# Sums of squares for a norm: adding the row blocks on VectorE before the product with ones, in the first pass of a streaming encoder step

## The chip, the cores and the metric

The kernel runs on one core of one Trainium2 chip. The metric is the device time of one execution in microseconds. TensorE (PE) multiplies matrices, VectorE (DVE), ScalarE (ACT) and GpSimd (POOL) work element by element, and SyncE (SP) issues the loads and stores (DMA).

## What is computed

The reference is one layer of a streaming encoder: 2048 prompt tokens and 8 x 16 sample tokens of width 1024. Each token is normalised, one projection feeds three groups of heads (forgetting attention, RWKV-7, cross-attention into 256 memory tokens), and a second projection brings the gated results back:

```
def rms_norm(x, g, eps=NORM_EPS):
    xf = x.astype(jnp.float32)
    y = xf * lax.rsqrt(jnp.mean(xf * xf, axis=-1, keepdims=True) + eps)
    return (y * g.astype(jnp.float32)).astype(x.dtype)
...
    h = rms_norm(x, norm_g) @ w_in
    fox_cols, rwkv_cols, mem_cols = jnp.split(h, [FOX_COLS, FOX_COLS + RWKV_COLS], axis=-1)
...
    y = x + o @ w_out
```

The change concerns `rms_norm` alone: how the sum of x² over the 1024 columns of a token is made.

## The kernel before

**Two phases.** The first (inside `with ExitStack() as p1`) goes over the tokens in four passes, `for it in range(4)`. Pass 0 takes 512 prompt tokens and the 128 sample tokens together, 640 columns; the passes 1 to 3 take 512 each. A pass normalises x (`prep_x`), projects it (`lora_in`, `shifted`, `wide`, `pair`), and runs the RWKV state update (`rwkv_in`, `rwkv_mid`, `rwkv_scan`, `rwkv_out`). The second phase does the two attentions and the output projection.

**The norm in pass 0.** x comes transposed, so that a tile holds 128 of the 1024 columns of x on its partitions and tokens along its free dimension; eight such row blocks (`raws[k]`, k = 0 to 7) make a token. `prep_x` goes over the 640 tokens in two parts, tokens 0 to 255 and 256 to 639 (`for t0, t1 in ((0, 2), (2, 5))`, in units of 128 tokens). For each part:

- L247 loads the blocks (SP; blocks 0 to 2 and 3 to 5 lie in two buffers of the weights' pool, tag `hl`; blocks 6 and 7 in the buffers `bk` and `bt`).
- L251 squares block k on ScalarE into the tile `xsq` (`sqs`).
- The product with `one1` (128 x 1 ones) on TensorE sums a block's squares over its 128 partitions. `xsq` is the stationary operand, so a product yields the sums of 128 tokens, one on each partition: column t of the PSUM tile `pq`. It is called through the helper `mm`, whose line is L59. Each fp32 product is two passes of TensorE in the trace.
- `rsqrt_small` makes the inverse root: scale and epsilon on VectorE (L68, out `rsq`), the power of -0.5 on GpSimd (L62).
- Products with `ident` spread the result over the partitions (`pb`, L59), and ScalarE copies it to `rb` (and, for the last 128 tokens, to `rb4`) at L269.
- For each block VectorE scales x by it and by the gain (L65, `xraw`), ScalarE rounds it to fp32r (L279, `xk`), and VectorE (even k) or GpSimd (odd k) forms the remainder (L62, `xk`). A value is kept as the sum of two such parts, and a projection takes three products for it.

Between the two parts the first weights are loaded (`between`): L200 loads, L201 rounds, GpSimd forms the remainder (`w`). The tiles of the pool `ws` with tag `hl`, four in all, hold these weights and, until the norm is done, also six of the eight blocks of x; the next weights (128x1024 for the columns k and r) go into the same four. `pjd` is the PSUM tile of the projections that `proj_d` makes. The passes 1 to 3 form the sums in another way (L261, ScalarE's accumulator over x in token order); the change doesn't touch these.

**What sets the order.** The program is written in one order, then put into another: `_arrange`, at the end of the kernel, gives each instruction a cost and its dependences, places all of the program's instructions on the five engines with a list scheduler that has fixed costs for each kind of instruction, for a slow array after a pause and for the buffers that a tile needs, and does so with three weights and six refinements of the ranks each. It keeps the order with the smallest computed total and sorts the whole program by it. Each engine then works through its instructions in that order, and waits for whatever each needs. Constant loads (L788, tile `craw`, with its conversions at L789) are part of the same order.

Of the kernel before, what the change touches and what calls it, by code (L numbers as in the profile page):

```python
# [17 lines left out]
KC = 8  # L18
# [33 lines left out]
def kernel(ctx: ExitStack, tc: tile.TileContext, I: dict, O: dict):  # L52
    nc = tc.nc
    V, S, G, PE, SY = nc.vector, nc.scalar, nc.gpsimd, nc.tensor, nc.sync
# [3 lines left out]
    def mm(out, lhsT, rhs, start=True, stop=True):  # L58
        PE.matmul(out, lhsT, rhs, start=start, stop=stop, skip_group_check=True)  # L59

    def tt(e, out, a, b, op):
        e.tensor_tensor(out=out, in0=a, in1=b, op=op)  # L62

    def stt(out, a, s, b, op0, op1):
        V.scalar_tensor_tensor(out=out, in0=a, scalar=s, in1=b, op0=op0, op1=op1)  # L65
# [9 lines left out]
    M, A_, SUB, MAX = ALU.mult, ALU.add, ALU.subtract, ALU.max  # L75
# [18 lines left out]
    def ct(name, shape, dtype=F32):  # L94
        return cp.tile(shape, dtype, tag=name, name=name)
# [15 lines left out]
    one1 = ct("one1", [128, 1])  # L111
# [6 lines left out]
    def rsqrt_small(out, ssum, n, scale, eps):  # L118
        ts(V, out, ssum, scale, eps, M, A_)
        tt(G, out, out, mhalf[:, :n], ALU.pow)  # L120


    with ExitStack() as p1:
# [93 lines left out]
        def spans(tok0, off, n):  # L217

            a = min(max(512 - off, 0), n)
            return [(o, m, t) for o, m, t in ((0, a, tok0 + off), (a, n - a, TP)) if m]  # L220

        def prep_x(tok0, n, xtok, xT, gcol, tiles=None, between=lambda: None):

            nt = n // 128
            first = n == 640
            ssq = sm.tile([128, 2, 8], F32, tag="ssq", name="ssq")
            rsq = sm.tile([128, 8], F32, tag="rsq", name="rsq")
            rb = xs_.tile([128, 512], F32, tag="rb", name="rb")
            rb4 = sm.tile([128, 512], F32, tag="nsq", name="rb4", bufs=1) if first else None
            xk, raws = [], []  # L230

            for t0, t1 in ((0, 2), (2, 5)) if first else ((0, nt),):
                c0, c1 = 128 * t0, 128 * t1
                if first:

                    m = c1 - c0
                    sqs = [rv.tile([128, 8, 256], F32, tag="gm", name="xsq", bufs=2)] if not t0 else [
                        rv.tile([128, 5, 384], F32, tag="gm", name="xsq", bufs=2), rv.tile([128, 3, 384], F32, tag="su", name="xsq2")]
                    pq = ps.tile([128, 512], F32, tag="ra", name="pq")
                    if not t0:  # L240
                        threes = [ws.tile([128, 2, 4, 256], F32, tag="hl", name="xraw").rearrange("p x a b -> p (x a b)")[
                            :, 0:1920].rearrange("p (k c) -> p k c", k=3) for _ in range(2)]
                        threes += [rv.tile([128, 1, 640], F32, tag=t_, name="xraw") for t_ in ("bk", "bt")]
                        raws = [threes[k // 3][:, k % 3] if k < 6 else threes[k - 4][:, 0] for k in range(KC)]
                    for j, k in enumerate((0, 3, 6, 7)):
                        for a, w, r0 in spans(tok0, c0, m):
                            SY.dma_start(threes[j][:, :, c0 + a:c0 + a + w],  # L247
                                         xT[128 * k:128 * (k + threes[j].shape[1]), r0:r0 + w].rearrange("(k p) t -> p k t", p=128))
                    for k in range(KC):
                        sq = sqs[k // 5 if t0 else 0][:, k % 5 if t0 else k, :]  # L250
                        S.activation(sq, raws[k][:, c0:c1], AF.Square)  # L251
                        for t in range(t1 - t0):
                            mm(pq[:, t:t + 1], sq[:, 128 * t:128 * t + 128], one1, start=k + t == 0, stop=k == KC - 1)
                    rsqrt_small(rsq[:, t0:t1], pq[:, 0:t1 - t0], t1 - t0, 1.0 / D, EPS)
                else:
                    for t in range(t0, t1):
                        r0 = tok0 + 128 * t
                        for j in range(2):
                            xt = xs_.tile([128, 512], F32, tag="xraw", name="xt", bufs=3)
                            SY.dma_start(xt, xtok[r0:r0 + 128, 512 * j:512 * j + 512])  # L260
                            S.activation(xt, xt, AF.Square, accum_out=ssq[:, j, t:t + 1])  # L261
                    tt(V, ssq[:, 0, :nt], ssq[:, 0, :nt], ssq[:, 1, :nt], A_)
                    rsqrt_small(rsq[:, t0:t1], ssq[:, 0, t0:t1], t1 - t0, 1.0 / D, EPS)
                pb = (ps if first else pj).tile([128, 512], F32, tag="ra" if first else "pj", name="pb")
                for t in range(t0, t1):
                    mm(pb[:, 128 * t - c0:128 * t - c0 + 128], rsq[:, t:t + 1].to_broadcast([128, 128]), ident)
                cuts = [(rb, 0, c0, min(c1, 512))] + ([(rb4, 512, 512, 640)] if c1 > 512 else [])
                for r_, o, a, b in cuts:
                    S.copy(r_[:, a - o:b - o], pb[:, a - c0:b - c0])  # L269
                for k in range(KC):  # L270
                    if not t0:
                        xk.append(tiles[k] if tiles else xs_.tile([128, 2, 640], F32R, tag="xk", name="xk", bufs=XKB))
                        if not first:
                            raws.append(xs_.tile([128, 512], F32, tag="xraw", name="xraw", bufs=3))
                            SY.dma_start(raws[k][:, :n], xT[128 * k:128 * (k + 1), tok0:tok0 + n])
                    raw, hl = raws[k], xk[k]
                    for r_, o, a, b in cuts:
                        stt(raw[:, a:b], raw[:, a:b], vec[:, gcol + k:gcol + k + 1], r_[:, a - o:b - o], M, M)
                    S.copy(hl[:, 0, c0:c1], raw[:, c0:c1])  # L279
                    tt(G if k % 2 else V, hl[:, 1, c0:c1], raw[:, c0:c1], hl[:, 0, c0:c1].bitcast(F32), SUB)  # L280
                if not t0:
                    between()
            return xk
# [566 lines left out]
        def memory_x():  # L850
            tiles = [rw.tile([128, 2, 256], F32R, tag=t_, name="xm") for t_ in ("e1", "e2", "e3", "e5", "xsk", "xsr")]
            tiles.append(rv.tile([128, 2, 256], F32R, tag="xsg", name="xm", bufs=2))
            tiles.append(rv.tile([128, 2, 256], F32R, tag="bv", name="xm", bufs=2))
            memx.extend(prep_x(0, 256, I["mem"], I["memT"], V_MG, tiles))
# [28 lines left out]
        for it in range(4):  # L883
            samp = it == 0
            tok0, n = 512 * it, 640 if samp else 512
            blocks = [(0, 256), (256, 384)] if samp else [(0, 512)]
            lora = []
            xk = prep_x(tok0, n, I["x"], I["xT"], V_G, between=lambda: lora.append(wd_load((LORA, 64), (FV + 384, 6))))
            lora_in(*lora, xk, blocks, it, tok0)
            if not it:  # L890
# [3 lines left out]
            nt, t0 = n // 128, 4 * it  # L894
# [1143 lines left out]
```

## Time and profile before

| | |
|---|---|
| three runs | median 1809.12 us (1807.52 to 1819.66) |
| the profiled execution | 1797.65 us |
| its span, first to last instruction | 1795.9 us |
| its mean granted TensorE clock | 0.972 |
| first start of a product with ones, last start | 4.6, 24.3 us |
| squares in pass 0 | 16 on ScalarE, 399 to 526 ns each |
| bytes moved in the first 60 us | 14.01 MB |

Times in the rows are microseconds from the start of the span unless marked ns. A row in order of time gives start, duration, engine, line, operation, out<-in with the tiles' names, shapes, how often it was merged, and in brackets how long the engine stood idle before it and what ended that. A row of a window gives the busy time of PE, of PE's weight loads, of DVE, ACT and POOL with their counts, then the granted clock (1.00 is full speed), the busy share of the DMA engines and the GB/s that they moved. A line in a row can be a helper's: L59 is every product, L62 every operation on two tensors, L65 and L68 those with a scalar.

### The profile page before, as it was taken

The page shows a single profiled execution, that of the slowest core. Times are in us where ns is not written, and L with a number is a line of the kernel's source. Part 1 is how long each engine was busy: PE and PEld are TensorE (multiplying, and loading weights), DVE is VectorE, ACT ScalarE, POOL GpSimd, SP SyncE. Part 2 cuts the span into 40 slices and gives each one's busy share as a digit, 9 for nine tenths or more (in the row PEclk, how much of TensorE's full clock was granted, in tenths as well). Part 3 has the DMA queues.
Part 4 walks back from the last instruction along what each step waited for, and adds up shares of the span by engine and source line. Part 5 has one row for each costly group of instructions (what it writes and reads, how often), then busy time and mean ns, then how long its engine had stood idle before and what let it go on. Part 6 is the DMA issues. An engine that isn't in the chain of part 4 may idle for free.

```text
span 1795.9 us, 41000 instructions
## 1 busy us (share of the span) xinstructions
PE 1696.7 (94%) x16313; PEld 1362.8 (76%) x16313; DVE 978.1 (54%) x2295; ACT 897.9 (50%) x1783; POOL 811.8 (45%) x824
## 2 busy tenths in 40 slices
PE   7989999999999999999899999799999899999998
PEld 6989989687887788886688887466667666667776
DVE  4654655572454564354574372776745765675214
ACT  5424343523243524233324343588898778886552
POOL 3654543242322242131132151477788566866552
PEclk8999999999999999999999999799999999999999
DMA  6763846653644654644635654534445772444432
GB/s 196 267 202 117 269 144 206 209 178 120 212 156 142 244 184 159 198 155 140 204 109 168 195 160 132 166 121 154 128 149 169 251 251 89 138 142 157 154 111 106
DMA packets 236314, 303.11 MB, mean 169 GB/s; under 512 B 81594, under 2 KB 185976, under 8 KB 220250
## 3 DMA queue, kind: packets, MB, share of 16 engines
q1 hardware_dynamic: 236122, 300.49, 51.5%
q8 instruction: 128, 2.10, 0.5%
q14 instruction: 64, 0.52, 0.1%
HBM read 210.15 MB, written 90.28 MB: 167 GB/s over the span
## 4 chain that ended last, share of the span: by engine, by line
PE 37%; DMA 7%; DVE 7%; ACT 7%; issue 2%; POOL 2%; SPq 1%; DVEq 0%; POOLq 0%; ACTq 0%
PE py L59 8%; PE po L59 6%; PE pjd L59 6%; PE pS L59 5%; PE pjt L59 3%; PE pm L59 2%; ACT P L1143 1%; DMA inv_d<-yt 1%; ACT Ph L1146 1%; POOL Pl L62 1%; DMA sp_d<-spr 1%; DMA xd<-inv_d 1%; DMA rb<-rd 1%; PE pz L59 1%; PE sc L59 1%
## 5 line engine op out<-in xcount | busy, mean ns | idle before, releaser
L59 PE MATMUL pjd<-xk,w 128*128 128x512 f32 (+4 forms) x2280 | 540.2, 378 | 13.0 <-ACT xk L279 4.6
L59 PEld LDWEIGHTS pjd<-xk,w 128*128 128x128 f32 (+1 forms) x2280 | 386.5, 192 | 80.8 <-issue 10.5
L62 POOL TENSOR_TENSOR Pl<-P,Ph 128x512 fp32r<-128x512 f32 (+3 forms) x272 | 318.8, 1183 | 160.6 <-ACT Ph L1146 132.8
L59 PE MATMUL pjt<-w,xk 128*128 128x256 f32 x2040 | 291.4, 290 | 3.9 <-issue 3.9
L59 PEld LDWEIGHTS pjt<-w,xk 128*128 128x128 f32 x2040 | 265.6, 192 | 10.1 <-issue 4.1
L59 PE MATMUL py<-W,oh 128*128 128x512 f32 x816 | 242.6, 399 | 0.9 <-ACT W L1331 0.4
L1143 ACT ACTIVATE P<-pS,NB 128x512 f32<-128x512 f32 x240 | 147.5, 624 | 87.1 <-PE pS L59 34.4
L59 PEld LDWEIGHTS py<-W,oh 128*128 128x128 f32 x816 | 150.9, 189 | 40.1 <-issue 1.0
L59 PE MATMUL pS<-Q,K 128*128 128x512 f32 x480 | 156.6, 387 | 7.1 <-ACT P L1143 4.7
L1146 ACT CAST Ph<-P 128x512 fp32r<-128x512 f32 (+3 forms) x272 | 150.7, 564 | 11.0 <-PE po L59 6.2
L59 PE MATMUL po<-Ph,vt 128*65 128x512 f32 x480 | 153.5, 371 | 2.6 <-ACT ob L1166 1.7
L59 PEld LDWEIGHTS pS<-Q,K 128*128 128x128 f32 x480 | 86.0, 193 | 45.4 <-ACT P L1143 21.6
L1087 DVE TENSOR_REDUCE mx<-pm 128x1 f32<-128x512 f32 x144 | 95.7, 685 | 25.1 <-PE pm L59 23.7
L62 POOL TENSOR_TENSOR nr<-nr,mhalf 128x8 f32<-128x8 f32 (+2 forms) x43 | 62.3, 1448 | 100.3 <-DVE nr L68 87.7
L62 POOL TENSOR_TENSOR w<-wraw,w 128x1024 fp32r<-128x1024 f32 (+1 forms) x34 | 81.6, 2411 | 46.2 <-ACT w L201 33.4
L59 PE MATMUL pm<-K,Q 128*128 128x512 f32 (+2 forms) x240 | 91.2, 399 | 9.2 <-DVE mx L1087 4.0
L59 PE MATMUL po<-Pl,vt 128*65 128x512 f32 x240 | 88.3, 369 | 3.1 <-POOL Pl L62 2.9
L62 DVE TENSOR_TENSOR xo<-py,xo 128x512 f32<-128x512 f32 x68 | 46.2, 685 | 77.9 <-PE py L59 77.6
L59 PEld LDWEIGHTS po<-Ph,vt 128*65 128x65 f32 x480 | 63.4, 136 | 30.9 <-ACT ob L1166 3.3
L62 DVE TENSOR_TENSOR ytmp<-yt 64x14 f32<-64x14 f32 (+9 forms) x210 | 55.0, 262 | 41.8 <-DMA yt<-ld 37.1
L718 ACT COPY qk<-pjt 128x512 f32<-128x512 f32 (+1 forms) x47 | 26.1, 564 | 97.0 <-PE pjt L59 96.7
L59 PEld LDWEIGHTS pm<-K,Q 128*128 128x128 f32 x240 | 46.1, 195 | 31.8 <-DVE mx L1087 11.3
(401 smaller groups left out, 2843.8 us busy)
## 6 DMA issues: line engine op xcount, KB each, us to landing
w<-w_d SPq DMA_DIRECT2D x84, 1024.0 KB
w_d<-w SPq DMA_DIRECT2D x28, 1024.0 KB
y_d<-xo SPq DMA_DIRECT2D x21, 512.0 KB
wraw<-in_w_in SPq DMA_DIRECT2D x36, 256.0 KB
xo<-in_x SPq DMA_DIRECT2D x17, 512.0 KB
xo<-y_d SPq DMA_DIRECT2D x17, 512.0 KB
xt<-in_x SPq DMA_DIRECT2D x24, 256.0 KB
xraw<-in_xT SPq DMA_DIRECT2D x24, 256.0 KB
```

Source lines behind the costliest of these rows:

```text
L59: PE.matmul(out, lhsT, rhs, start=start, stop=stop, skip_group_check=True)
L62: e.tensor_tensor(out=out, in0=a, in1=b, op=op)
L718: S.copy(o_, out)
L1087: V.tensor_reduce(out=to, in_=pm[:, :n], op=MAX, axis=AX.X)
L1143: S.activation(P_[:, c0:], pS[:, c0:], AF.Exp, bias=NB[:, qb, 2 * hp + h, kt:kt + 1] if fox else 0.0)
L1146: S.copy(Ph[:, c0:], P_[:, c0:])
```

## The change

The eight squared blocks are added up on VectorE, each into block 0's tile in place, as soon as the block is squared. The products with ones follow once all eight are in: one for 128 tokens instead of eight. In pass 0 this makes two products in the first part (was 16) and three in the second (was 24), and adds seven additions of 128x256 and seven of 128x384. The sum has another order of additions, fp32 throughout. `tt(V, out, a, b, A_)` is a `tensor_tensor` addition on VectorE.

```
                     for k in range(KC):
                         sq = sqs[k // 5 if t0 else 0][:, k % 5 if t0 else k, :]
                         S.activation(sq, raws[k][:, c0:c1], AF.Square)
-                        for t in range(t1 - t0):
-                            mm(pq[:, t:t + 1], sq[:, 128 * t:128 * t + 128], one1, start=k + t == 0, stop=k == KC - 1)
+                        if k:
+                            tt(V, sqs[0][:, 0, :], sqs[0][:, 0, :], sq, A_)
+                    for t in range(t1 - t0):
+                        mm(pq[:, t:t + 1], sqs[0][:, 0, 128 * t:128 * t + 128], one1, start=t == 0)
                     rsqrt_small(rsq[:, t0:t1], pq[:, 0:t1 - t0], t1 - t0, 1.0 / D, EPS)
```

## Prediction

> **What bounds the kernel now.** I first read the busy times of the page and its span in 40 slices, then the windows, then the instructions in order of time in the first 60 us, where the whole change lies.
>
> ```profile
> span 1795.9 us, 41000 instructions
> PE 1696.7 (94%) x16313; PEld 1362.8 (76%) x16313; DVE 978.1 (54%) x2295; ACT 897.9 (50%) x1783; POOL 811.8 (45%) x824
> PE   7989999999999999999899999799999899999998
> ```
> ```profile
> core 0: us, PE busy (x) PEld busy (x) DVE busy (x) ACT busy (x) POOL busy (x), PEclk, DMA share, GB/s
> 0.00:60.00 60.00, 45.23 (x220) 41.37 (x221) 32.52 (x74) 33.11 (x81) 26.38 (x35) 0.89 0.76 234
> 60.00:700.00 640.00, 610.66 (x7507) 532.41 (x7506) 338.58 (x810) 237.23 (x502) 237.24 (x240) 0.98 0.56 184
> 700.00:800.00 100.00, 98.67 (x1304) 83.54 (x1304) 49.90 (x113) 31.27 (x61) 27.14 (x33) 1.00 0.55 175
> 800.00:900.00 100.00, 90.11 (x927) 67.02 (x926) 49.68 (x176) 36.63 (x85) 17.84 (x24) 0.92 0.53 169
> ```
>
> TensorE is the bound of the whole: 1651 of the 1736 us after the first 60 are PE work. A start that is earlier by so much brings the end forward by about as much, if nothing else gives way. The first 60 us are another matter: PE stands for 14.8 us there, and part of its work is the product with ones. So I read that stage in order of time.
>
> ```profile
> start us, us, engine line op out<-in xcount [idle before <-releaser]
> 4.10 1.03 ACT L251 ACTIVATE xsq<-xraw 128x256 f32<-128x256 f32 x3 [2.07 <-DMA xraw<-in_xT]
> 4.57 6.98 PE L59 MATMUL pq<-one,xsq 128*128 128x1 f32 x32 [4.57 <-ACT xsq L251]
> 5.46 1.64 ACT L251 ACTIVATE xsq<-xraw 128x256 f32<-128x256 f32 x5 [0.33 <-DMA xraw<-in_xT]
> 8.23 1.35 ACT L251 ACTIVATE xsq<-xraw 128x384 f32<-128x384 f32 x3 [1.14 <-DMA xraw<-in_xT]
> 10.10 0.52 ACT L251 ACTIVATE xsq<-xraw 128x384 f32<-128x384 f32 x1 [0.52 <-DMA xraw<-in_xT]
> 11.59 0.16 DVE L68 TENSOR_SCALAR rsq<-pq 128x2 f32<-128x2 f32 x1 [10.40 <-PE pq L59]
> ...
> 14.12 1.76 ACT L251 ACTIVATE xsq<-xraw 128x384 f32<-128x384 f32 x4
> 14.25 1.28 DVE L65 SCALAR_TENSOR_TENSOR xraw<-xraw,vec,rb 128x256 f32<-128x256 f32 x3 [2.51 <-ACT rb L269]
> 14.27 10.40 PE L59 MATMUL pq<-one,xsq 128*128 128x1 f32 x48 [0.46 <-ACT rb L269]
> ...
> 24.54 1.75 PE L59 MATMUL pjd<-xk,w 128*70 128x256 f32 x7
> 24.71 0.16 DVE L68 TENSOR_SCALAR rsq<-pq 128x3 f32<-128x3 f32 x1 [1.62 <-PE pq L59]
> 24.96 0.87 POOL L62 TENSOR_TENSOR rsq<-rsq,mhalf 128x3 f32<-128x3 f32 x1 [3.23 <-DVE rsq L68]
> 26.08 1.48 PE L59 MATMUL pb<-ident,rsq 128*128 128x128 f32 x6
> 27.22 2.34 PE L59 MATMUL pjd<-xk,w 128*70 128x256 f32 x17
> 27.62 0.30 ACT L789 CAST reset<-craw 128x128 bf16<-128x128 f32 x1 [7.63 <-DMA craw<-in_reset]
> ...
> 28.37 1.02 DVE L62 TENSOR_TENSOR WUP<-uraw,WUP 32x384 fp32r<-32x384 f32 x2 [3.49 <-ACT WUP L797]
> ...
> 31.20 0.52 ACT L269 COPY rb<-pb 128x256 f32<-128x256 f32 x2
> 31.59 3.47 DVE L65 SCALAR_TENSOR_TENSOR xraw<-xraw,vec,rb 128x256 f32<-128x256 f32 x8 [2.20 <-ACT rb L269]
> ...
> 33.74 0.40 PE L59 MATMUL pjd<-xk,w 128*70 128x384 f32 x1 [4.18 <-ACT xk L279]
> ```
>
> The reader is to see three things. The squares of the first part (256 tokens) end at 7.10 (5.46 + 1.64), their sums on PE only at 11.55: PE is late by 4.45 us, and VectorE stands for 10.40 us until then. The second part (384 tokens) is held longer: its last square ends at 15.88, its sums at 24.67. Behind it stand the inverse root on GpSimd, the product pb, the copy rb on ScalarE and the scaling on VectorE, which begins at 31.59. The copy rb does not follow at once: ScalarE takes its work in order, and a conversion ahead of it waited 7.63 us for a load.
>
> **The change part by part.** *Removed on PE.* Each fp32 product is two passes in the trace: 40 products, 80 passes. From first to last start the 32 passes take (6.98 - 0.35) / 31 = 0.214 us each, the 48 the same, (10.40 - 0.35) / 47. Ten passes stay (two and three products), 70 go: 15.0 us of PE time. That is the most that PE's work alone can give back; it counts only where PE, not data, was the limit.
>
> *Added on VectorE.* Seven additions of 128x256 and seven of 128x384, each waiting for its square and for the addition before it. Rows for such an operation:
>
> ```profile
> 34.98 0.55 DVE L62 TENSOR_TENSOR xk<-xraw,xk 128x384 fp32r<-128x384 f32 x1
> ```
> ```profile
> L62 DVE TENSOR_TENSOR xk<-xraw,xk 128x384 fp32r<-128x384 f32 x4 | 4.7, 1205 | 1.4 <-ACT xk L279 1.4
> L62 DVE TENSOR_TENSOR xk<-xraw,xk 128x256 fp32r<-128x256 f32 x4 | 3.6, 945 | 0.0
> ```
>
> One 384-wide subtraction took 0.55; the mean of four is 1.205, which I put down to GpSimd's work beside them. For 256 columns the low end is 0.37 (0.55 x 256/384), the high end 0.945. The first part's additions fall between 4.8 and 8 us, where GpSimd has no work (the fifth busy figure):
>
> ```profile
> 4.50:7.20 2.70, 2.63 (x13) 2.64 (x13) 0.00 (x0) 2.26 (x8) 0.00 (x0) 1.00 1.12 347
> ```
>
> GpSimd's next work is the inverse root behind rsq. I take 0.43 there, which is also the pace of the scalings of that width (3.47 / 8). By the second square, at about 4.85, the chain can start: 4.85 + 7 x 0.43 = 7.9, and four passes (3 x 0.214 + 0.35) end at 8.9 instead of 11.55. **First lead: 2.65 us.** At 0.945 it would be 4.85 + 6.6 + 1.0 = 12.5, a loss of 0.9; at 0.37 the last square rules, 7.10 + 0.37 + 1.0 = 8.5, a lead of 3.05.
>
> *The second part.* Behind the first sum VectorE is busy without a break, then nearly idle until rb comes:
>
> ```profile
> 14.25:22.96 8.71, 8.69 (x41) 8.69 (x41) 8.71 (x24) 5.74 (x17) 5.15 (x6) 1.00 0.56 160
> 22.96:31.59 8.63, 6.60 (x39) 6.34 (x38) 1.31 (x5) 3.07 (x9) 0.87 (x1) 1.00 0.72 229
> ```
>
> The busy stretch moves 2.65 forward, to end at 20.3. Of the seven wide additions three fit before it (their squares end at 9.58 to 10.62); four go into it, 4 x 0.55 = 2.2. With the 1.18 of small work in the gap (1.02 and 0.16), VectorE is free for the second part at 20.3 + 2.2 + 1.2 = 23.7 instead of 31.59: **7.9 us earlier.** Is its input there? From the start of rsq (24.71) to the end of pb (27.56) is 2.85, rb another 0.52. If the additions end by 18, six passes (5 x 0.214 + 0.35 = 1.4) and these 3.4 put rb at about 22.8, in time. What would be late next is VectorE itself. If ScalarE's order keeps rb behind the late load, only the first lead is left, and if that load does not move, nothing. So the lead of the second part lies between 0 and 7.9; I take 7, near the upper end, because the whole order is worked out anew from the new dependences and rb need not stay behind that conversion.
>
> [...]
>
> *Does the lead pass on?* The scaled second part frees the buffers in which x lay, and these are what the weights of the next projections are converted into:
>
> ```profile
> 38.50 1.04 ACT L201 CAST w<-wraw 128x1024 fp32r<-128x1024 f32 x1
> ...
> 51.11 6.18 PE L59 MATMUL pjd<-xk,w 128*128 128x384 f32 x39 [0.90 <-DVE fl L62]
> ```
> ```profile
> 51.00:57.30 6.30, 6.18 (x39) 6.01 (x39) 5.42 (x7) 3.29 (x7) 3.69 (x4) 1.00 1.04 410
> ```
>
> The DMA engines are full in 51 to 57, at 410 GB/s; the 60 us as a whole carry 234 GB/s, 14.0 MB. In 53 us that would be 264, well under 410. So loads need not stop a lead of 7, though they can take some of it. After 60 PE has work all the time, and the lead stays.
>
> *Sum.* 1797.65 (the profiled execution, span 1795.9) - 7 = 1790.6. The three runs have a median of 1809.12, 11.5 above that execution; against them the forecast is **1802 us**, with 1797 to 1807 for this case. Moving PE's 15 us of work in full would be the far end, 1794.
>
> **The rivals.**
>
> *The lead is spent on the way* (gain 0 to 3, 1808). For it: the 7.63 us wait of ScalarE for a load, with rb behind it, and DMA engines that are full in 51 to 57. Against it: rb can be put ahead of the conversion, and PE is idle enough to take earlier work. What the changed program does not do is leave the products in place; that the additions come late on VectorE belongs here.
>
> *The clock falls earlier* (gain 3.7, 1805.4). The trace shows what a pause of PE does to the granted clock:
>
> ```profile
> 29.56:33.74 4.18, 0.00 (x0) 0.00 (x1) 2.15 (x7) 2.98 (x10) 0.39 (x1) 1.00 0.65 214
> 34.40:47.50 13.10, 10.92 (x40) 8.69 (x41) 11.04 (x18) 9.62 (x21) 9.02 (x7) 0.50 0.62 200
> 42.00:47.50 5.50, 5.48 (x25) 5.30 (x25) 4.88 (x4) 2.90 (x7) 5.39 (x4) 0.50 0.87 270
> ```
>
> After 4.18 us of pause the clock was 0.50 for 13.1 us, the last 5.5 with PE busy all the time. The change opens such a pause earlier, between 9 and some 16 us, with only the four passes of pb in it, since the ones products that filled it are gone. Then the 24 pjd passes of the first part, 0.138 each at full clock (2.34 / 17), take 0.276: 3.3 us more, and 7 - 3.3 = 3.7. Against it: those passes wait for xk one by one, so that half clock may cost nothing there; and if the pause at 29.56 closes, the spell of 13.1 us, worth 6.5 us of PE time, goes, which leads to the fourth case. [...]
>
> *The new order is worse later* (slower: 1819). The order of all engines is computed for the whole program, and other dependences in its first 30 us can give another order after it. Its price: the stretch 800 to 900 has 90.11 us of PE work, the one before it 98.67, 8.6 us lost to chains that PE waits for. One more such stretch takes the lead; from there it decides: two are 7 - 17.2 = 10 slower. Against it: a lead alone does not change what follows, and PE is full in most slices of the page.
>
> *PE's work comes through in full* (1794 or less). The 15.0 us are won where PE was the limit until 24.67, and the half-clock spell shortens. Against it: VectorE's 23.7.
>
> **How the numbers follow.** The forecast has 0.45; the lead spent 0.17, the clock 0.10, the worse order 0.15, the full 15 us 0.13. The range runs to the middle of the outer cases, with room for a new order in either direction: 1789 to 1817. A change of 1% is 18 us, about what a measurement of this kernel can tell from none, since its three runs spread over 12. Faster than 1791 needs the fourth case and a better order besides: 0.10. Slower than 1827 needs three worse stretches: 0.05. Within 1%: 0.85.
>
> **What would show it.** Ten pq passes instead of 80; rsq of the first part at 8.9 to 9.2 instead of 11.59; additions at about 0.43 and 0.55; the scaling of the second part at 23 to 25 instead of 31.59; the first 128x1024 weight conversion near 31 instead of 38.50; the same amount of PE work after 60. I am wrong if rb stays near 31 behind a conversion, if the additions run at 0.9 or more, or if PE's pauses after 60 us, 84 us now, change by more than the lead.

## The result, and the profile after

| | before | after |
|---|---|---|
| median of 11 runs each, on one chip | 1810.21 us (1806.72 to 1819.66) | 1797.6 us (1783.06 to 1803.33) |
| ratio, 95% interval | | 0.9919 (0.9894 to 0.9944) |
| profiled execution, its span | 1797.65, 1795.9 us | 1797.69, 1795.7 us |
| its mean granted clock | 0.972 | 0.977 |

The change makes the kernel 14.7 us faster (0.0081 x 1810.21; 10.1 to 19.2 by the interval; the medians differ by 12.6). The forecast was 7 us, a time of 1802, between 1789 and 1817. The two profiled executions are equal to 0.04 us: that of before happens to lie below all of its eleven timed runs. Laid side by side, these two traces would say "no change"; the timed runs say otherwise.

From the page of after, its span and its busy times:

```profile
span 1795.7 us, 40894 instructions
PE 1678.9 (94%) x16243; PEld 1347.8 (75%) x16243; DVE 980.9 (55%) x2309; ACT 895.5 (50%) x1783; POOL 803.5 (45%) x824
```

70 PE passes fewer and 14 VectorE operations more: the change does what it says. The windows of after:

```profile
0.00:60.00 60.00, 29.46 (x116) 23.75 (x117) 38.26 (x86) 32.16 (x75) 24.99 (x32) 0.89 0.67 211
60.00:300.00 240.00, 233.41 (x2744) 221.21 (x2743) 133.96 (x277) 93.94 (x192) 125.18 (x112) 0.99 0.61 203
```

PE stands for 60 - 29.46 = 30.5 us of the first 60; before it was 14.8. Nothing else has moved into the time that the sums left free: PE has done 116 passes by then, and in before it had done 220, of which 150 (220 - 70) are passes that both kernels have. By this count the new kernel is 34 passes behind at 60 us. The start of after in order of time:

```profile
7.42 1.65 ACT L251 ACTIVATE xsq<-xraw 128x384 f32<-128x384 f32 x4 [1.12 <-DMA xraw<-in_xT]
...
11.10 1.01 PE L59 MATMUL pq<-one,xsq 128*128 128x1 f32 x4 [11.10 <-DVE xsq L62]
...
20.54 1.65 PE L59 MATMUL pb<-ident,rsq 128*128 128x128 f32 x6 [0.26 <-POOL rsq L62]
...
24.52 0.51 ACT L799 CAST WUP<-uraw 32x384 fp32r<-32x384 f32 x1 [5.92 <-DMA uraw<-in_w_up]
...
27.33 0.36 ACT L271 COPY rb<-pb 128x256 f32<-128x256 f32 x1
27.82 3.94 DVE L65 SCALAR_TENSOR_TENSOR xraw<-xraw,vec,rb 128x256 f32<-128x256 f32 x8
...
34.96 1.03 ACT L201 CAST w<-wraw 128x1024 fp32r<-128x1024 f32 x1
...
42.25 7.05 PE L59 MATMUL pjd<-xk,w 128*70 128x384 f32 x32 [4.88 <-POOL xk L62]
...
55.41 6.80 PE L59 MATMUL pjd<-xk,w 128*128 128x384 f32 x33 [5.84 <-DVE xsk L65]
```

The first sum ends at 12.11 (11.10 + 1.01), later than the 11.55 of before and far from 8.9; among the squares ScalarE waits 1.12 us for a load. The second part is scaled from 27.82, 3.8 us earlier than before, and the first weight conversion stands at 34.96, 3.5 earlier. But PE then waits 4.88 us for a remainder on GpSimd and 5.84 us for a scaling on VectorE. By the count of passes above PE is behind at 60 us, not ahead. And the order of all engines is another one, from the first loads to the end. So two things have changed at once: the sums, and the order. The experiments separate them.

### The profile page after: what moved, and what is told of

Same layout as the page of the kernel before. It is cut to its first block, busy times and chain, and to the rows that moved or that the text cites. A ratio compares the mean times of both kernels' runs of the same rounds, so it can differ in the third digit from the quotient of the medians.

```text
span 1795.7 us, 40894 instructions
## 1 busy us (share of the span) xinstructions
PE 1678.9 (94%) x16243; PEld 1347.8 (75%) x16243; DVE 980.9 (55%) x2309; ACT 895.5 (50%) x1783; POOL 803.5 (45%) x824
## 4 chain that ended last, share of the span: by engine, by line
PE 40%; DMA 7%; DVE 5%; ACT 5%; issue 3%; POOL 2%; SPq 1%; DVEq 0%; POOLq 0%; ACTq 0%
PE py L59 9%; PE po L59 7%; PE pjd L59 6%; PE pS L59 5%; PE pjt L59 3%; PE pm L59 2%; POOL Pl L62 2%; ACT P L1145 1%; DMA w<-w_d 1%; DMA inv_d<-yt 1%; DMA xd<-inv_d 1%; DMA AR<-sp_d 1%; DMA sp_d<-spr 1%; PE sc L59 1%; ACT Ph L1148 1%
## 5 line engine op out<-in xcount | busy, mean ns | idle before, releaser
L59 PE MATMUL pjd<-xk,w 128*128 128x512 f32 (+5 forms) x2280 | 547.8, 379 | 26.4 <-DMA w<-w_d 7.3
L59 PE MATMUL pjt<-w,xk 128*128 128x256 f32 x2040 | 298.4, 290 | 0.0
L59 PEld LDWEIGHTS pjt<-w,xk 128*128 128x128 f32 x2040 | 271.3, 193 | 10.7 <-issue 4.0
L59 PE MATMUL pS<-Q,K 128*128 128x512 f32 (+1 forms) x480 | 157.1, 384 | 10.0 <-ACT P L1145 6.5
```

## The experiments

An order is taken over from one kernel to another by writing it out: at the end of `_arrange`, the search gives way to a list that holds a rank for every instruction. "Order as a list" below stands for this edit:

```
-    for w, stay in _TRIES:
-        rank = p.emitted(w)
...
-    _, start = min(found, key=lambda x: x[0])
...
+    for i, d in zip(prog[0], struct.unpack("<%dH" % (len(raw) // 2), raw)):
+        r = (r + d) & 0xFFFF
+        at[i.name] = r
```

"Old order" is that of the kernel before and "new order" that of the kernel after; operations that exist in one of them only take the place of those that they stand for. Ratios are against the kernel before on the same chip; 1% is 18 us.

### e1: the kernel before, unchanged

> The kernel before, unchanged, to see a second profiled execution of it and what a comparison with itself gives. Both theories (L: the gain is the earlier sums in the first pass; O: the gain comes from the order that was computed anew for all that follows) expect no difference, within 5 us. The first profiled execution of the kernel before took 1797.65 us, below every one of its eleven runs (1806.72 to 1819.66): I expect the second nearer 1810, and its PE pauses after 60 us above the 84 us of the first.

Measured: 0.9997 (0.9967 to 1.0028). The profiled execution took 1812.91 us at a mean clock of 0.970, 15 us more than the one of before, with the same instructions; PE's pauses after 60 us come to 94.5 us, against 84 in before. A difference of this size between two single traces says nothing.

### e2: the new sums in the old order

The diff of the change, and the old order as a list.

> The additions on VectorE and one product per 128 tokens, with every other instruction in the order of the kernel before (the order is written out in the kernel; an addition stands where the last product of its block stood). L expects most of the gain: 10 to 15 us faster. O expects little of it: between 4 us faster and 3 slower, since the copy rb still stands behind the conversion that waits for its load at 27.62.

Measured: 1.0006 (0.9981 to 1.0032): the sums by themselves, placed like this, bring nothing that can be measured. The windows of e2:

```profile
0.00:60.00 60.00, 32.20 (x165) 28.41 (x165) 38.26 (x91) 34.55 (x83) 26.04 (x35) 0.91 0.76 232
60.00:300.00 240.00, 225.72 (x2695) 213.81 (x2695) 136.12 (x268) 91.16 (x185) 124.27 (x109) 0.99 0.59 197
```

In before the second window was:

```profile
60.00:300.00 240.00, 229.63 (x2720) 217.14 (x2719) 137.18 (x278) 92.60 (x186) 125.92 (x110) 0.99 0.59 197
```

PE has 32.20 us of work instead of 45.23 in the first 60, and 27.8 us of idle time instead of 14.8. Without the 70 passes, e2 is 15 passes ahead of before at 60 us (165 and 150). At 300 us it has done 2860, between the two executions of before (220 + 2720 - 70 = 2870, and 2855 in e1). So in the same order a small lead at 60 us is gone by 300. Where PE's idle time lies, in order of time:

```profile
4.98 3.61 DVE L62 TENSOR_TENSOR xsq<-xsq 128x256 f32<-128x256 f32 x7 [3.80 <-ACT xsq L251]
...
8.65 1.01 PE L59 MATMUL pq<-one,xsq 128*128 128x1 f32 x4 [8.65 <-DVE xsq L62]
...
15.77 1.08 DVE L62 TENSOR_TENSOR xsq<-xsq 128x384 f32<-128x384 f32 x1
...
20.24 0.55 DVE L62 TENSOR_TENSOR xsq<-xsq 128x384 f32<-128x384 f32 x1
...
23.45 1.13 DVE L62 TENSOR_TENSOR xsq<-xsq,xsq 128x384 f32<-128x384 f32 x2
...
24.73 1.41 PE L59 MATMUL pq<-one,xsq 128*128 128x1 f32 x6 [12.80 <-DVE xsq L62]
...
26.00 1.75 PE L59 MATMUL pjd<-xk,w 128*70 128x256 f32 x7
...
26.71 0.30 ACT L791 CAST reset<-craw 128x128 bf16<-128x128 f32 x1 [6.29 <-DMA craw<-in_reset]
...
27.54 1.49 PE L59 MATMUL pb<-ident,rsq 128*128 128x128 f32 x6
...
28.68 3.22 PE L59 MATMUL pjd<-xk,w 128*70 128x256 f32 x17
29.67 0.63 ACT L263 ACTIVATE xt<-xt 128x512 f32<-128x512 f32 x1 [0.90 <-DMA xt<-in_x]
...
30.30 0.52 ACT L271 COPY rb<-pb 128x256 f32<-128x256 f32 x2
30.69 2.72 DVE L65 SCALAR_TENSOR_TENSOR xraw<-xraw,vec,rb 128x256 f32<-128x256 f32 x8 [2.22 <-ACT rb L271]
...
38.38 1.04 ACT L201 CAST w<-wraw 128x1024 fp32r<-128x1024 f32 x1
```

The first lead is there: the sum ends at 9.66, 1.9 us ahead of before. The second sum ends at 26.14, 1.5 us *behind* before (24.67), because the old order strews the wide additions through VectorE's busy stretch, the last at 23.45. The product pb then ends at 29.03, yet rb comes only at 30.30: ScalarE stands 6.29 us for the load `craw`, SyncE issues the load `xt` behind that conversion, at 27.03, and ScalarE waits for `xt` too before it gets to rb. In before the same row was

```profile
30.57 0.63 ACT L261 ACTIVATE xt<-xt 128x512 f32<-128x512 f32 x1 [0.88 <-DMA xt<-in_x]
```

with craw at 27.62, pb's end at 27.56 and rb at 31.20. Craw, xt and rb are all 0.9 us earlier in e2, and pb is 1.5 later: rb follows the loads, not the sum. The weight conversion is where it was, 38.38 against 38.50. This is the rival of the prediction in which the lead is spent on the way, and its own reason, rb behind the late load, is these rows.

### e3: the old sums in the new order

The kernel before, and the new order as a list.

> The eight products per 128 tokens of the kernel before, with every other instruction in the order of the changed kernel (the products of the first part stand where the additions stood, those of the second where the three products stood). L expects it no faster than the kernel before, 0 to 8 us slower, as the second sum again takes 10 us of PE. O expects most of the gain: 5 to 15 us faster.

Measured: 0.9927 (0.9900 to 0.9954), 13 us faster, with all 80 passes of the old sums in place. So the whole gain is there without the change's arithmetic. In order of time:

```profile
17.93 10.40 PE L59 MATMUL pq<-one,xsq 128*128 128x1 f32 x48 [3.14 <-ACT rb L269]
...
39.11 1.04 ACT L201 CAST w<-wraw 128x1024 fp32r<-128x1024 f32 x1
...
47.02 5.74 PE L59 MATMUL pjd<-xk,w 128*70 128x384 f32 x32 [6.02 <-POOL xk L62]
```

Within the new order the new sums do win time at the start: 34.96 against 39.11 at the conversion, 42.25 against 47.02 at the long row of products, that is 4 to 5 us. At the end 1.4 us of it can be seen (0.9927 - 0.9919), with an uncertainty of some 7. Together the four kernels are a table of two by two:

| ratio to before | old order | new order |
|---|---|---|
| old sums | 0.9997 | 0.9927 |
| new sums | 1.0006 | 0.9919 |

Down a column nothing that can be told from zero, along a row 0.7 to 0.9%.

### e5, e6 and e7: where in the program the order gains

All three have the new sums and an order as a list: e5 the new one for the first phase and the old for the second, e6 the other way round, e7 the old one for the first 60 us and the new for the rest.

> The changed sums; the first phase (the four passes) in the order of the changed kernel, the second phase (attentions and output projection) in that of the kernel before. Theory P1 (the better order is that of the first phase) expects 10 to 15 us faster than the kernel before; theory P2 (it is that of the second phase) expects 0 to 5 us faster. The profiles so far put the kernels with the new order 2 us ahead at 1100 us, and 8 at the end, with a scatter of several us: I lean to P2.

> The changed sums; the first phase in the order of the kernel before, the second in that of the changed kernel. P1 expects 0 to 5 us faster than the kernel before, P2 expects 8 to 15 us faster.

> The changed sums; what both orders place in the first 60 us stands in the order of the kernel before, all else in that of the changed kernel. Both profiles with the new order are 6 to 8 us behind at 60 us and level again at 300. If that start is a loss that stays, this kernel is 16 to 22 us faster than the kernel before; if what was late at 60 us is caught up in any case, it is as fast as the changed kernel, 10 to 16 us faster than before.

Measured: e5 0.9970 (0.9946 to 0.9995), e6 0.9970 (0.9945 to 0.9995), e7 0.9888 (0.9854 to 0.9922). Either phase gives 5.4 us (1 to 10), somewhat under half of the 13 us that the order is worth, so neither theory was right: P1 expected all of it from the first phase, P2, to which I leaned, from the second. With the old order in the first 60 us the gain grows to 20 us: by the ratios the new order's start costs some 5, though e7's interval and that of after overlap (with the old sums, e3 and e10 below, it is 12, and their intervals don't). The windows of e7 beside those of after, above, say the same in passes:

```profile
0.00:60.00 60.00, 29.87 (x155) 26.51 (x156) 38.83 (x90) 33.34 (x82) 26.65 (x35) 0.94 0.75 237
60.00:300.00 240.00, 231.83 (x2752) 219.34 (x2750) 136.94 (x279) 92.61 (x188) 123.47 (x110) 1.00 0.61 201
```

At 60 us e7 is 39 passes ahead of after (155 and 116), at 300 us 47. So here, between two kernels with the same order from 60 us on, a lead at the start does stay. e2 too is 49 passes ahead of after at 60, but has lost them at 300 (165 + 2695 = 2860 = 116 + 2744): the old order is slower there. (A count of passes compares orders only roughly, since passes are of several lengths: in before 0.21 us for one of pq, 0.14 for one of pjd with 256 columns.)

### e10: the old sums in e7's order

The kernel before, and the mixed order of e7 as a list.

> The eight products per 128 tokens of the kernel before in the order with the old start and the new rest. If the order alone counts: 16 to 22 us faster than before, as with the changed sums. If the changed sums have a part in it: 8 to 14 us faster.

Measured: 0.9859 (0.9822 to 0.9897), a median of 1784.08 against 1809.61. This is the fastest kernel of the study, 25 us ahead of before, and it doesn't contain the change. Against e7 the intervals overlap, so the old sums aren't shown to be better.

### e4, e8, e11 and e12: other orders from the same search

The search tries three weights and six refinements of each. e4 leaves a weight out for the kernel before, and so gets its next order; e11 leaves it the weight 0.3 alone; e8 and e12 do the like with the kernel after.

```
e4   -_TRIES = ((0.3, 0), (0.45, 0), (0.6, 0))   +_TRIES = ((0.3, 0), (0.45, 0))
e11  -_TRIES = ((0.3, 0), (0.45, 0), (0.6, 0))   +_TRIES = ((0.3, 0),)
e8   -_AGAIN = 6                                 +_AGAIN = 5
e12  -_TRIES = ((0.3, 0), (0.45, 0), (0.6, 0))   +_TRIES = ((0.45, 0), (0.6, 0))
```

> The kernel before with another order of the same instructions: the third of the three weights for which orders are computed is left out (_TRIES has two), so that the best of the twelve other candidates is taken. Nothing else differs. L expects it within 5 us of the kernel before. O expects that an order by itself moves the time by 5 to 15 us, either way.

> The changed kernel with another order of the same instructions: the sixth refinement of the ranks is left out (_AGAIN is 5), and the best of the fifteen other candidates is taken. L (earlier sums give the gain) expects the gain of the changed kernel, 10 to 15 us faster than before. O (one order happens to be good) expects a time of its own, between 5 us faster and 8 us slower than before.

> The kernel before with orders computed for the first of the three weights alone (_TRIES = (0.3, 0)); both orders of the changed sums that ran 13 to 15 us faster came from this weight, those of the old sums that ran within 3 us of each other from the other two. If the weight is what matters: 9 to 16 us faster than before. If each order is a draw of its own: between 6 us faster and 6 slower.

> The changed kernel with orders computed for the second and third weight alone. If the changed sums allow better orders whatever the weight: 9 to 16 us faster than before. If the weight or a lucky draw is what matters: between 6 us faster and 6 slower.

Measured: e4 0.9986 (0.9959 to 1.0013), e8 0.9925 (0.9896 to 0.9954), e11 0.9931 (0.9906 to 0.9956), e12 0.9985 (0.9960 to 1.0011). By the weight of the order that was taken:

| | old sums | new sums |
|---|---|---|
| weight 0.3 | e11 0.9931 | after 0.9919, e8 0.9925 |
| weight 0.45 or 0.6 | before 1, e4 0.9986 | e12 0.9985 |

Over these six orders the gain goes with the weight, not with the sums. Alone, e4 and e8 had come out as theory L (the earlier sums give the gain) expected; e11 and e12 decide against it. The kernel before could have had 12.5 us of the gain by leaving two of the three weights out of `_TRIES`, and the change without the weight 0.3 has none of it that can be told from zero. The order of e11 was among the candidates for before all along, and by the computed total the search put both the order of before and that of e4 ahead of it; on the chip e11 is the fastest of the three. What the changed sums did was to tip the search from one family of orders to another. Why the orders of weight 0.3 are better was not found, and there are only three orders of each kind.

### e9: the forecast lead, put in by hand

e7, with the additions of the second part placed right behind their squares and everything from its sum on some 7 us earlier (order as a list, edited).

> As the kernel with the old start and the new rest (20 us faster than before), with the step that the forecast relied on put in by hand: the seven wide additions stand right behind their squares, the second sum, its inverse root, pb and rb right behind them, everything of the second part and of the first weights 7 us earlier in the order than the constants' conversions and the loads for the next pass. If the lead passes on (the forecast's step), the scaling of the second part begins near 21 to 24 us instead of 31, and the kernel is 5 to 8 us faster than that one, 25 to 28 faster than before. If the lead is spent at loads and at GpSimd, the scaling comes earlier and the time stays within 3 of that kernel, 17 to 23 faster than before.

Measured: 0.9908 (0.9873 to 0.9943), inside e7's interval. In order of time:

```profile
23.89 3.20 DVE L65 SCALAR_TENSOR_TENSOR xraw<-xraw,vec,rb 128x256 f32<-128x256 f32 x7 [2.20 <-ACT rb L271]
...
30.65 1.05 ACT L201 CAST w<-wraw 128x1024 fp32r<-128x1024 f32 x1 [1.00 <-issue]
...
31.92 2.63 DVE L62 TENSOR_TENSOR WUP<-uraw,WUP 32x384 fp32r<-32x384 f32 x1
...
34.59 2.98 DVE L65 SCALAR_TENSOR_TENSOR xraw<-xraw,vec,rb 128x128 f32<-128x128 f32 x3
...
37.52 0.63 ACT L263 ACTIVATE xt<-xt 128x512 f32<-128x512 f32 x1 [2.10 <-DVE xraw L65]
...
45.95 0.63 ACT L263 ACTIVATE xt<-xt 128x512 f32<-128x512 f32 x1 [2.64 <-DMA xt<-in_x]
...
48.30 0.35 PE L321 MATMUL pf<-ident,fsb 6*128 6x6 f32 x3 [2.02 <-ACT fsb L318]
...
49.55 7.78 PE L59 MATMUL pjd<-xk,w 128*128 128x384 f32 x39 [0.90 <-DVE fl L62]
```

The early steps come out as forecast: scaling at 23.89 (23.7 said), conversion at 30.65 (31 said). The next links break. GpSimd begins the weights' remainders at 31.78 (39.62 in before), and beside it VectorE takes 2.63 us for one small remainder and 2.98 for three scalings of 128x128; ScalarE waits 2.10 for the last of these. Later ScalarE waits 2.64 for a load `xt`, and PE 2.02 for a copy of ScalarE behind it. The row of 39 products starts at 49.55. In before it started at 51.11: the lead of 7.85 us at the conversion (38.50 - 30.65) is down to 1.56 there. The same row starts at 50.28 in e7, whose conversion stands at 37.50, and at 49.55 in e2, where no lead was forced. At 60 us e9 has done 138 passes, e7 155. Whether a better hand-made place for the later work would have kept it was not tried.

### What the new order does better in the second phase

From the first product `pS` to the end of the span, the profiled executions take:

| second phase by weight | us |
|---|---|
| 0.45 or 0.6: before, e1, e2, e4, e5, e12 | 653.2, 656.3, 656.1, 654.1, 654.9, 661.6 |
| 0.3: after, e3, e6, e7, e8, e9, e10, e11 | 647.4, 648.1, 649.0, 648.4, 650.1, 645.2, 646.8, 652.3 |

The groups don't overlap, and their means are 656.0 and 648.4; but e11 lies only 0.9 us below before, and two executions of one program (before and e1) differ by 3.1. Between the old order and the new one, the stretch from about 400 to 480 us after the first `pS` holds a part of the difference. In e1 (old order) the windows of it, two of 10 us and the whole, and the PE rows with a wait of more than 0.4 us:

```profile
1584.00:1594.00 10.00, 7.58 (x40) 5.35 (x39) 9.35 (x27) 6.45 (x15) 4.18 (x7) 0.91 0.44 141
1594.00:1604.00 10.00, 10.00 (x39) 7.14 (x38) 4.44 (x11) 8.99 (x18) 6.19 (x8) 0.75 0.28 80
1554.00:1634.00 80.00, 74.78 (x398) 53.09 (x396) 55.45 (x127) 67.53 (x128) 59.02 (x61) 0.94 0.37 117
```
```profile
1589.76 0.47 PE L59 MATMUL pm<-K,Q 128*128 128x512 f32 x1 [0.71 <-issue]
1590.71 0.62 PE L59 MATMUL pS<-Q,K 128*128 128x384 f32 x2 [0.48 <-ACT P L1143]
...
1593.19 0.69 PE L59 MATMUL pS<-Q,K 128*128 128x128 f32 x2 [0.84 <-ACT P L1143]
```

The same in after:

```profile
1578.00:1588.00 10.00, 8.97 (x51) 6.45 (x49) 4.05 (x13) 9.19 (x19) 6.60 (x10) 1.00 0.64 209
1588.00:1598.00 10.00, 9.41 (x42) 6.34 (x42) 8.57 (x20) 9.71 (x18) 8.24 (x8) 1.00 0.58 173
1548.00:1628.00 80.00, 76.74 (x426) 55.41 (x426) 58.98 (x131) 70.57 (x132) 61.45 (x61) 1.00 0.47 155
```

In the old order PE stands for 2.42 of 10 us there, in short pauses, and the granted clock goes to 0.75 in the next 10 us, in which PE is busy all the time. In the new one the pauses are 1.03 and the clock stays at 1.00. (Pauses of the same size don't always do it: from 1624 to 1634 PE of e1 stands for 2.05 us, 0.48 and 0.93 of it within 2.5, at a clock of 1.00.) The 80 us hold 398 passes in e1 and 426 in after. The kernels with one order for each phase show that it goes by the order of this phase, e5 (old) and e6 (new):

```profile
1540.00:1620.00 80.00, 75.17 (x410) 53.97 (x409) 56.53 (x130) 69.44 (x131) 60.24 (x62) 0.96 0.37 118
```
```profile
1551.00:1631.00 80.00, 76.85 (x428) 55.34 (x427) 57.11 (x130) 70.63 (x134) 61.93 (x62) 1.00 0.47 158
```

18 to 28 passes at 0.18 to 0.19 us each (76.74 / 426, 74.78 / 398) are 3 to 5 us, by an estimate that takes all passes as equal. This tells the old order from the new one, not one weight from the other: e11, of weight 0.3, has 411 passes in its stretch, and e12, of the others, 419 at a clock of 1.00 and yet the longest second phase. That the pauses make the clock fall is my reading of this sequence and was not shown: no run took them away alone, and from 1554 to 1574 the clock of e1 is 0.88 and then 0.95 with 0.52 us of pause in the 20, after 0.84 in the 10 before. The rest of the second phase and the half that e5 gains in the first phase weren't located: the first phase ends between 1134.7 and 1154.8 us in these executions, and the same program scatters by 12 us there (before 1142.7, e1 1154.8).

## Why the prediction was right or wrong

The time was forecast well enough, 1802 against 1797.6 and inside the range; the reason given for it was wrong, so that this is luck. The range of 28 us also holds 1810.21, the time of before, and the gain of 14.7 is twice the 7 that the lead was to give.

- **Work on PE.** Ten pq passes instead of 80: right, as is "the same amount of PE work after 60" (1678.9 - 29.46 = 1649.4, before 1696.7 - 45.23 = 1651.5; pauses 86 us instead of 84, where the same program has 84 and 94.5 in two executions).
- **First lead, 2.65.** In the old order 1.9 (e2). The mis-sized term is the addition: seven took 3.61, 0.52 each, where 0.43 was taken from the scalings. In the kernel after the lead is -0.6 (12.11 against 11.55), since its order mixes the additions of both parts and ScalarE waits for a load among the squares.
- **Second lead, 7.** Not found in either order: 0.9 at the scaling in the old one (30.69 against 31.59), 3.8 in the new. Two terms failed. One is the wait of rb, which set the start in e2: "rb need not stay behind that conversion" was a guess. In e2 rb stays behind it and behind the load `xt`, whose issue waits for the conversion, and comes 1.27 us after pb's end. In the kernel after ScalarE stands 5.92 us for another load (24.52), and rb comes at 27.33, although pb ended at 22.19. The other is the place of the wide additions. They were to stand together and early; the old order has the last at 23.45, so that without the loads rb could have come at about 29 at best, not at 22.8. Their price is a small part: in e2 two of the seven took 1.08, with GpSimd at work from 14.68 to 19.17 beside them, and five about 0.55, four of them with GpSimd idle, 1.1 us more than the low row for all.
- **The lead passes on.** This is the step that failed. Even with the second lead forced, as forecast to 0.4 us (e9), no gain in time follows: 7.85 us at the conversion are 1.56 at the row of 39 products. "After 60 the lead stays" holds between e7 and after; e2's lead of 15 passes over before at 60 us is gone at 300.
- **The rivals.** *The lead is spent on the way* (0.17) is what happens to the sums: e2 has a gain of -1 (-6 to 3) us. *The new order is worse later* (0.15) named the right actor with the wrong sign: another order for the whole program is what moved the time, by about 13 us, to the better. Its price of 8.6 us for one bad stretch is near the 7.6 between the second phases, but was read from another stretch. I gave no chance to a better order except as an addition to the fourth rival. *PE's work in full* was refuted by PE's idle time in the first 60 us. *The clock falls earlier* cost little: in e2 PE stands 12.80 us before the second sum, and the 24 pjd passes of the first part then take 4.97 us (1.75 + 3.22) against 4.09 in before, 0.9 more and not 3.3; the mean clock of its first 60 us is 0.91 against 0.89.

## What to carry to other kernels

Where an order is computed anew for the whole program, a local edit is two changes: test the arithmetic in the old order and the old arithmetic in the new one before crediting either. Work taken off the busiest engine, in a stage where that engine waited for data, brought only what the next link could take: 70 passes fewer left PE 34 passes behind at 60 us in the new order and 15 ahead in the old one, with no gain at 300. Ask for the last link of the chain, not for the engine's share. And compare timed runs before traces: where runs of one program scatter by more than the effect, two single profiles can show any sign.

## What the runs showed that was not expected

- One program, one core, and yet 20 us of scatter: the kernel before ran in 1795.29 us at a mean granted clock of 0.978 and in 1817.05 at 0.969, on one chip.
- A cluster of PE pauses of 0.5 to 0.9 us, 2.42 us in 10 together, was followed by a granted clock of 0.75 over 10 us of full work (e1, above), while 2.05 us of pauses 40 us later were not; the prediction had weighed single pauses of several us only.
- Orders from one search differ by 0.7% on the chip, and by 1.4% with a start from another order (e10): more than the arithmetic that was to be judged.
